# The opening of a decoder trunk kernel: x loaded and normalized ahead of the first modulation weights, those weights in groups of 4, 2 and 2 chunks, weight units split by rows instead of columns, and a shorter chain for the decay rates

## The chip, the cores and the metric

The kernel runs on one core of one Trainium2 chip. The metric is the device time of one execution in microseconds; smaller is better. The time before is the median of three runs, 1262.42 us (1261.84 to 1265.04).

## The reference: what is computed

One inference step of a two-layer decoder trunk on 576 token rows of width 1024: a prompt of 512 rows and 8 samples of 8 rows. All tensors are float32. Around the change, only the beginning matters:

```
def modulate(h, shift, scale):
    return h * (1 + scale[:, None, :]) + shift[:, None, :]

sh1, sc1, g1, sh2, sc2, g2 = split(silu(c) @ ada_w[l] + ada_b[l], 6)    # c: 9 rows (1 prompt, 8 samples)
h = modulate(rms_norm(x, norm_g[l, 0]), sh1, sc1)
xr, yg = split(h @ rnn_w_in, 2)                                          # 1024 x 2048
xr, new_buf = causal_dwconv(xr, conv_buf, conv_w, conv_b)                # width 4
g = einsum('btnc,ncd->btnd', xr blocks, gate_w) + gate_b                 # 8 blocks of 128 x 256
log_a = 8 * sigmoid(g_r) * log_sigmoid(lam)                              # lam: the decay rates, 1024 numbers
...                                                                      # scan, gelu branch, w_out, residual, SwiGLU, attention, SwiGLU
```

So nothing of the first large product, `h @ rnn_w_in`, can be finished before the shift and scale of layer 0 are known for all 1024 features, and these need 2 x 1024 x 1024 numbers of `ada_w` (8.4 MB).

## The kernel before, in words

**Tiling.** Features stand on the 128 partitions, in `KC` = 8 chunks `c` of 128; tokens run along the free dimension in two halves `h` = 0, 1 of 288 columns (256 of the prompt, 32 of the samples). A large product is split into a high and a low part of both operands: per chunk of 128 features three matmuls of 128x128 weights with 128x288 columns (`product`). One output column block of 128 features in one half is 24 such matmuls into one PSUM bank, tile `mm`. There are 6 banks `mm` and 2 banks `ada`. The modulated activations stand in a tile `h` per half, high and low part.

**Weights.** A `Unit` is 512 KB of weights. `load_more` issues its DMA into a `raw` tile (4 of these); `convert` makes the high part on ScalarE (`CAST wh<-raw`) and the low part on VectorE (`TENSOR_TENSOR wh<-raw,wh`) into two `wh` tiles (10 of these). Before, a unit of `rnn_w_in` is one column block with all 8 chunks of rows, in runs of 512 bytes; the two units of the gate weights are each one half of every block's columns.

**The opening.** `x_load` issues the DMAs of the five x tiles (the samples, 4 tiles of 128 prompt rows) into `reg` tiles (5 of these). `x_half(h)` sums the squares, makes the reciprocal root (`acc`, after `spread`), and turns the x tiles with TensorE into `x[h]`. The shift and scale weights of layer 0 come in four groups of two chunks. `ada_first_load(c, ...)` issues 8 DMAs of 256 KB for a group, `ada_first(c)` multiplies them with silu(c) (`cz`, 9 columns padded to 32) in 32 matmuls of 128 columns into a bank `ada`, turns the result with TensorE (`mm<-ident,ta`), and adds the bias into `mods` (`ada_end`). `modulated` then does, chunk by chunk and half by half: normalize (`ta<-x,acc`), scale and shift on ScalarE (`ACTIVATE tb<-ta,mods`), high part on ScalarE (`CAST h<-tb`), low part on VectorE or GpSimd (`h<-tb,h`). The x tiles of half 1 are loaded behind the first group of weights and turned after its modulation. `decay_rates` computes softplus of `lam` with a range reduction, a polynomial and a series: some 90 small VectorE instructions on 128x8 numbers (`sl<-sl`).

**Order.** The program is first recorded as a list of operations. A planner (`Recorder.schedule`) then places them with its own costs and wait times, earliest possible start first, lower program position preferred (`early(n)` moves a piece n positions ahead), and fixes the order of the instructions on each engine: TensorE (PE), VectorE (DVE), ScalarE (ACT), GpSimd (POOL) and the DMA issues on SyncE (SP). On the chip each engine follows that order strictly, so an instruction that waits holds all that stand behind it. Since the planner issues everything, nearly every row of the profile has the one line L447 (L453 in the changed kernel). Rows are told apart by their tiles. The names there: `reg` x tiles or modulation weights, `wh` weight parts or modulation weights, `raw` loaded units, `ada<-wh,cz` and `ada<-reg,cz` modulation products, `mm<-h,wh` the products of h with `rnn_w_in`, `mm<-ident,..` turns.

## Time and profile before

| | |
|---|---|
| median of 3 runs | 1262.42 us |
| the profiled execution's own time | 1263.01 us |
| its span | 1261.2 us, 1.8 us less than its time |
| TensorE busy | 1237.8 us (98%) |
| VectorE, ScalarE, GpSimd busy | 920.3, 663.1, 252.7 us |
| DMA | 165.38 MB, 131 GB/s over the span |
| first product of h, `mm<-h,wh` | begins at 20.71 us |
| first 512-column modulation product, `ada<-reg,cz` | begins at 56.87 us |

Times in the trace count from the start of the span. A row of the timeline gives start, length, engine, operation, tiles, how often it repeats and, in brackets, the engine's idle time before it with what ended it. Lengths of matmuls overlap, since they are pipelined; the distance from start to start is the rate. A float32 matmul (the modulation products) stands in the trace as two records. The windows view gives, for stretches of time, busy us and number of records of each engine, the granted TensorE clock (1.00 is full), the share of the DMA engines and the GB/s moved.

### The profile page before, as it was taken

To read this page: it belongs to the slowest core of one execution; us is meant where nothing else is said; L and a number is where in the kernel's file an instruction comes from. 1 tells how busy PE (TensorE), PEld (TensorE's weight loads), DVE (VectorE), ACT (ScalarE), POOL (GpSimd) and SP (SyncE) were. 2 spreads that over 40 slices of the span, in tenths; PEclk is the share of its full clock that TensorE was granted. 3 is DMA by queue.
4 is the path that set the end of the run, shared out by engine and by line. 5 is a ranking of instruction groups with operands and counts; after the bars stand their busy time and mean duration, and the time that the engine had idled before them with its cause. 6 is when DMAs were issued, how large, how long until landed. Compare 5 with 4: busy or idle time off the path is not lost.

```text
span 1261.2 us, 25276 instructions
## 1 busy us (share of the span) xinstructions
PE 1237.8 (98%) x9532; PEld 1166.9 (93%) x9532; DVE 920.3 (73%) x2283; ACT 663.1 (53%) x1498; POOL 252.7 (20%) x542
## 2 busy tenths in 40 slices
PE   7999999999999999999999999999999999999997
PEld 5798999899899899989998997999999999999997
DVE  6998784795577468656778887558957865875776
ACT  4788973764255335514567678538523542552442
POOL 3456351101100010011024335100011011001011
PEclk8999999999999999999999999999999999999999
DMA  9955554535456655464513220332342232332322
GB/s 306 318 179 188 188 177 151 170 86 171 140 152 191 185 167 184 156 194 137 167 33 75 68 60 27 111 97 97 85 133 68 84 110 76 90 100 80 100 69 76
DMA packets 219755, 165.38 MB, mean 131 GB/s; under 512 B 23629, under 2 KB 204841, under 8 KB 219602
## 3 DMA queue, kind: packets, MB, share of 16 engines
q1 hardware_dynamic: 219186, 163.45, 43.0%
q8 instruction: 75, 1.23, 0.4%
q0 software_dynamic: 448, 0.32, 0.1%
q14 instruction: 46, 0.38, 0.1%
HBM read 160.85 MB, written 4.87 MB: 131 GB/s over the span
## 4 chain that ended last, share of the span: by engine, by line
PE 86%; DVE 6%; ACT 4%; DMA 2%; POOL 1%; issue 1%; SPq 0%; ACTq 0%; DVEq 0%
PE mm L447 82%; PE ada L447 4%; DVE wh L447 1%; DVE ta L447 1%; ACT tb L447 1%; DVE sl L447 1%; ACT ta L447 1%; DVE tb L447 1%; ACT h L447 1%; DMA raw<-in_rnn_w_in_dram 1%; ACT wh L447 1%; POOL h L447 1%; DMA reg<-in_ada_w_dram 1%; ACT sl L447 1%; DMA reg<-in_x_prompt_dram 1%
## 5 line engine op out<-in xcount | busy, mean ns | idle before, releaser
L447 PE MATMUL mm<-h,wh 128*128 128x288 f32 x4128 | 596.2, 298 | 3.8 <-ACT h L447 1.8
L447 PEld LDWEIGHTS mm<-h,wh 128*128 128x128 f32 x4128 | 560.5, 188 | 23.2 <-issue 11.3
L447 PE MATMUL mm<-sl,wh 128*128 128x288 f32 x3218 | 460.6, 296 | 0.4 <-ACT sl L447 0.3
L447 ACT CAST wh<-raw 128x512 fp32r<-128x512 f32 (+2 forms) x380 | 269.1, 721 | 345.7 <-PE mm L447 208.9
L447 PEld LDWEIGHTS mm<-sl,wh 128*128 128x128 f32 x3218 | 436.6, 188 | 9.0 <-issue 5.9
L447 DVE TENSOR_TENSOR wh<-raw,wh 128x512 fp32r<-128x512 f32 (+2 forms) x380 | 310.2, 828 | 59.3 <-ACT wh L447 57.0
L447 DVE SCALAR_TENSOR_TENSOR x<-mm,mods,x 128x256 f32<-128x256 f32 x160 | 77.0, 482 | 136.1 <-PE mm L447 136.0
L447 POOL TENSOR_TENSOR td<-td,td 128x288 f32<-128x288 f32 x38 | 35.5, 934 | 475.8 <-ACT td L447 467.7
L447 POOL TENSOR_TENSOR x<-x,ta 128x32 f32<-128x32 f32 x152 | 55.3, 364 | 331.1 <-DVE ta L447 325.9
L447 PE MATMUL mm<-tb,wh 128*128 128x288 f32 (+1 forms) x488 | 88.5, 296 | 0.4 <-ACT td L447 0.4
L447 PEld LDWEIGHTS mm<-tb,wh 128*128 128x128 f32 x488 | 72.4, 188 | 1.9 <-DVE sl L447 0.8
L447 ACT COPY td<-mm 128x288 f32<-128x288 f32 (+2 forms) x140 | 49.0, 364 | 37.7 <-DVE mm L447 18.0
L447 DVE TENSOR_TENSOR raw<-raw,raw 128x512 f32<-128x512 f32 x76 | 61.4, 808 | 0.9
L447 PE MATMUL mm<-ta,wh 128*128 128x288 f32 (+1 forms) x254 | 56.1, 298 | 0.0
L447 ACT ACTIVATE ta<-x 128x288 f32<-128x288 f32 x56 | 24.8, 444 | 55.6 <-POOL x L447 52.4
L447 DVE TENSOR_TENSOR raw<-raw 128x512 f32<-128x512 f32 x76 | 52.2, 688 | 1.1
L447 DVE TENSOR_TENSOR td<-mm,td 128x288 f32<-128x288 f32 x76 | 34.5, 454 | 23.4 <-PE mm L447 23.3
L447 PE MATMUL ada<-reg,cz 128*32 128x512 f32 (+1 forms) x448 | 49.5, 553 | 0.0
L447 PEld LDWEIGHTS mm<-ta,wh 128*128 128x128 f32 x254 | 41.7, 188 | 1.8 <-ACT wh L447 0.8
L447 ACT ACTIVATE ta<-ta,stat 128x128 f32<-128x128 f32 (+2 forms) x72 | 32.3, 471 | 18.5 <-DVE stat L447 17.7
L447 DVE TENSOR_TENSOR acc<-acc,ta 128x288 f32<-128x288 f32 x54 | 25.1, 464 | 12.4 <-ACT ta L447 12.4
L447 ACT CAST sl<-ta 128x288 fp32r<-128x288 f32 x54 | 23.0, 431 | 18.5 <-DVE ta L447 18.5
(202 smaller groups left out, 1197.9 us busy)
## 6 DMA issues: line engine op xcount, KB each, us to landing
raw<-in_ffn_w_in_dram SPq DMA_DIRECT2D x88, 512.0 KB
reg<-in_ada_w_dram SPq DMA_DIRECT2D x80, 512.0 KB
raw<-in_ffn_w_out_dram SPq DMA_DIRECT2D x48, 384.0 KB
raw<-in_rnn_w_in_dram SPq DMA_DIRECT2D x16, 512.0 KB
reg<-in_kv_ada_w_dram SPq DMA_DIRECT2D x16, 512.0 KB
wh<-in_ada_w_dram SPq DMA_DIRECT2D x24, 256.0 KB
raw<-in_rnn_w_out_dram SPq DMA_DIRECT2D x8, 512.0 KB
raw<-in_ffn_w_out_dram SPq DMA_DIRECT2D x8, 512.0 KB
```

Source lines behind the costliest of these rows:

```text
L447: self.rec.add(eng, lambda: getattr(obj, name)(*map(real, args), **{k: real(v) for k, v in kw.items()}), cost, outs, ins, func, lat, port, ...
```

## The change

- All five x tiles are loaded first; both halves are turned and normalized before any modulation weight is needed. The normalized chunks are kept in 18 `sl` tiles (`X0`), and `modulated` starts from them (`known=True`).
- The first modulation weights come in groups of 4, 2 and 2 chunks (`FIRST`). The group of 4 comes in 8 DMAs of 512 KB with runs of 2 KB, and is multiplied in 32 matmuls of 256 columns; the others as before in 32 matmuls of 128 columns each. A group's matmuls are bound together in three batches (`FQ`: the row quarters 0 and 1, then 2, then 3), so that the planner puts nothing between those of one batch. The result is turned in a bank `ada` (`own`), not `mm`.
- The `rnn_w_in` units of x0 to x3 each hold two column blocks and half the rows (`unit_two`, runs of 1 KB; job `linear_two`). The two gate units each hold both halves of four blocks (1 KB runs), so the first can be dropped earlier.
- `decay_rates` uses ScalarE's Exp and fused operations: 21 or 22 instructions.
- The planner's costs for DMAs now depend on the run length, and one for the modulation matmuls changes.

```diff
-ST = (1, 1, 1)
-EW = EP = EA = EK = E1 = ER = 0
+ST = (2, 1, 2)
+CONV = (1, 1, 1)
+KIND = (0, 1, 0)
+FQ = ((0, 1), (2,), (3,))
+FIRST = ((0, 4), (4, 2), (6, 2))
+EW = EP = EA = EK = ER = 0
+E1 = ((400, 200), (0, 0), (0, 0))
...
-    for t in (4, 0, 1):
+    for t in (4, 0, 1, 2, 3):
         x_load(t)
...
     def decay_rates():
...
-        for kk in (64, 32, 16, 8, 4, 2, 1):
...
-        for n in range(11, 0, -1):
...
+        V.tensor_tensor(p_, lamT, neg, ALU.min)
+        S.activation(p_, p_, AF.Exp)
...
+        for n in range(15, 1, -2):
+            V.scalar_tensor_tensor(s_, s_, 1.0 / n, w2, ALU.add, ALU.mult)
...
-    def ada_first(c):
+    def ada_first(c, n):
         o = ps(pada, "ada")
-        for q, b in enumerate(first_w[c]):
-            for k in range(2):
-                ada_mm(o, 2 * q + k, [b.f[:, n : n + P] for n in (256 * k, 256 * k + P, 512 + 256 * k, 512 + 256 * k + P)], q + k == 0, q + k == 4)
-            b.done()
-        t = ada_turn(o, 1)[:, 0:P].rearrange("p (g c b) -> p g c b", g=2, c=2)
...
+        w = n * P // 2
+        for qs in FQ:
+            with rec.together():
+                for q, k in ((q, k) for q in qs for k in range(2)):
+                    bs = first_w[c][q]
+                    ada_mm(o, 2 * q + k, [bs[g % len(bs)].f[:, (512 * g) % (1024 // len(bs)) + (2 * k + i) * w :][:, 0:w] for g in (SH1, SC1) for i in range(2)], q + k == 0, q + k == 4)
...
+        t = ada_turn(o, n // 2, True)[:, 0 : n * P // 2].rearrange("p (i g f b) -> p g f i b", i=n // 2, g=2, f=2)
...
+    ug = [Unit(KC, [(ALL, slice(0, 4), ALL2, gw[4 * j : 4 * j + 4].rearrange("n p d -> p n d"))]) for j in range(2)]
...
+    def linear_two(us, col, ops, evac):
+        def run(h):
+            o = ps()
+            product(o[:, 0:HC], us[0], ops(h)[0:4], last=False, col=col)
+            product(o[:, 0:HC], us[1], ops(h)[4:8], first=False, col=col)
+            with early(ER):
+                evac(h, o)
+        jobs.append(Job(0.369 * KC, run, us, us))
...
+        if w[0] == "x" and c < 4:
+            if c % 2 == 0:
+                pair[c] = tuple(unit_two(w_in, c * P, k, 4) for k in (0, 4))
+            linear_two(pair[c - c % 2], c % 2 * P, hops, evac_xr(c))
...
+        X0[h] = [sl() for _ in range(KC + 1)]
+        V.tensor_tensor(X0[h][KC].f[:, 0 : 32 * KC].rearrange("p (c n) -> p c n", c=KC), x[h][:, :, HP:HC], rstd[h][:, HP:HC].unsqueeze(1).to_broadcast([P, KC, 32]), ALU.mult)
+        for c in range(KC):
+            (V, V, G)[c % 3].tensor_tensor(X0[h][c].f[:, 0:HP], x[h][:, c, 0:HP], rstd[h][:, 0:HP], ALU.mult)
...
     x_half(0)
-    ada_first_load(0, whs)
+    x_half(1)
+    load_more(1)
+    ada_first_load(*FIRST[0], whs)
     vectors()
-    load_more(1)
-    for t in (2, 3):
-        x_load(t)
     H[0], H[1] = hkind[0](F32R), hkind[1](F32R)
-    for c in range(0, KC, 2):
-        if c < 6:
+    for i, (c, n) in enumerate(FIRST):
+        if CONV[i]:
             convert()
-        ada_first(c)
-        if c < 6:
-            load_more(ST[c // 2])
-            ada_first_load(c + 2, (whs, regs, whs)[c // 2])
+        ada_first(c, n)
+        if i + 1 < len(FIRST):
+            ada_first_load(*FIRST[i + 1], (whs, regs)[KIND[i + 1]])
+            load_more(ST[i])
         for h in range(2):
-            with early(E1):
-                modulated(h, SC1, SH1, M1, slice(c, c + 2))
-            if c == 0 and h == 0:
-                x_half(1)
+            with early(E1[i][h]):
+                modulated(h, SC1, SH1, M1, slice(c, c + n), X0[h], True)
```

How the change moves instructions shows at two places. The first is SP's queue of DMA issues after the first two x tiles. Before (a row `128x2x256 x2` is two DMAs of 256 KB; `x_prompt` rows are 512 KB, `rnn_w_in` rows 512 KB):

```order
L447 DMA reg_111<-in_x_prompt_dram 128x1024
L447 DMA reg_113<-in_x_prompt_dram 128x1024
L447 DMA sl_116<-in_ada_b_dram 96x128
L447 DMA sl_118<-in_norm_g_dram 32x128
L447 DMA wh_121<-in_ada_w_dram 128x2x256 x2
L447 DMA wh_127<-in_ada_w_dram 128x2x256 x2
L447 DMA wh_137<-in_ada_w_dram 128x2x256 x2
L447 DMA wh_147<-in_ada_w_dram 128x2x256 x2
L447 DMA raw_160<-in_rnn_w_in_dram 128x8x128
L447 DMA reg_166<-in_x_prompt_dram 128x1024
L447 DMA reg_173<-in_x_prompt_dram 128x1024
```

Now:

```order
L453 DMA reg_107<-in_x_prompt_dram 128x1024
L453 DMA reg_109<-in_x_prompt_dram 128x1024
L453 DMA reg_112<-in_x_prompt_dram 128x1024
L453 DMA reg_114<-in_x_prompt_dram 128x1024
L453 DMA sl_117<-in_ada_b_dram 96x128
L453 DMA sl_120<-in_norm_g_dram 32x128
L453 DMA raw_124<-in_rnn_w_in_dram 128x4x256
L453 DMA wh_131<-in_ada_w_dram 128x2x512
L453 DMA wh_135<-in_ada_w_dram 128x2x512
L453 DMA wh_140<-in_ada_w_dram 128x2x512
L453 DMA wh_146<-in_ada_w_dram 128x2x512
```

Two more x tiles and a unit now stand ahead of the first modulation weights, and four more rows like the last follow (8 DMAs of 512 KB in place of 8 of 256 KB), then the group of chunks 4 and 5 (2.1 MB), two units, and the group of chunks 6 and 7. Up to and with the last modulation weight of the opening, three units stand in this queue now; before there were three of `rnn_w_in` and one of the gates.

The second place is TensorE's order around the last modulation group of the opening. Before (`ada_661` is that group's bank, `mm_349`, `mm_398` and so on are column blocks of `rnn_w_in`):

```order
L447 MATMUL ada_661<-wh_385,cz 32x128 x6
L447 MATMUL mm_349<-h_323,wh_314 128x288
L447 MATMUL ada_661<-wh_446,cz 32x128 x2
L447 MATMUL mm_398<-h_323,wh_383 128x288
L447 MATMUL mm_349<-h_323,wh_314 128x288
L447 MATMUL mm_349<-h_323,wh_325 128x288
L447 MATMUL ada_661<-wh_446,cz 32x128 x6
L447 MATMUL mm_349<-h_323,wh_314 128x288
L447 MATMUL ada_661<-wh_470,cz 32x128 x2
L447 MATMUL mm_349<-h_323,wh_314 128x288
```

Now:

```order
L453 MATMUL ada_585<-wh_351,cz 32x128 x8
L453 MATMUL ada_585<-wh_361,cz 32x128 x8
L453 MATMUL mm_441<-h_432,wh_523 128x288
L453 MATMUL mm_444<-h_432,wh_523 128x288
L453 MATMUL mm_552<-h_432,wh_539 128x288 x2
L453 MATMUL mm_441<-h_432,wh_523 128x288
L453 MATMUL mm_441<-h_432,wh_537 128x288
L453 MATMUL mm_441<-h_432,wh_523 128x288
L453 MATMUL mm_444<-h_432,wh_523 128x288
```

The modulation matmuls of a group stood in pieces of 2 and 6 between single products of h; now 16 stand together, and the other 16 in a second batch further on. Counted in the order, 122 products of h stand ahead of the first 512-column modulation matmul before, and 135 now. Of the modulation matmuls of 128 columns, 96 of the 128 stood behind the first product of h; now 48 do, in batches of 8, 8, 16 and 16, besides 16 more (and the 32 of 256 columns) ahead of it.

83 lines of the change are left out of this document (44 added, 39 removed).

## The prediction

> **What bounds the kernel now.** First the page: the span, TensorE's share, and the slices.
>
> ```profile
> span 1261.2 us, 25276 instructions
> PE 1237.8 (98%) x9532; PEld 1166.9 (93%) x9532; DVE 920.3 (73%) x2283; ACT 663.1 (53%) x1498; POOL 252.7 (20%) x542
> ...
> PE   7999999999999999999999999999999999999997
> ...
> PEclk8999999999999999999999999999999999999999
> DMA  9955554535456655464513220332342232332322
> ```
>
> TensorE is the bound except in the first slice, where the DMA engines are full, and the last, which the change doesn't touch. The windows view by stage says the same:
>
> ```profile
> 0.00:60.00 60.00, 49.15 (x466) 36.09 (x467) 46.46 (x194) 34.99 (x82) 20.58 (x50) 0.94 1.03 311
> 60.00:200.00 140.00, 139.61 (x1047) 127.53 (x1046) 117.70 (x247) 110.63 (x208) 69.48 (x164) 1.00 0.57 182
> ```
>
> From 60 us on TensorE stands still for 0.4 us in 140, and 1047 records in 140 us are 0.134 us each. What the change can bring is therefore the time at which the opening hands over to this saturated stretch. TensorE's timeline of the opening:
>
> ```profile
> 9.31 1.56 PE L447 MATMUL mm<-ident,reg 128*128 128x128 f32 x8 [0.17 <-DMA reg<-in_x_prompt_dram]
> ...
> 19.56 1.06 PE L447 MATMUL mm<-ident,reg 128*128 128x128 f32 x8 [1.75 <-DMA reg<-in_x_prompt_dram]
> 20.71 0.61 PE L447 MATMUL mm<-h,wh 128*128 128x288 f32 x1
> ...
> 34.81 0.66 PE L447 MATMUL mm<-h,wh 128*128 128x288 f32 x3 [1.57 <-ACT h L447]
> ...
> 44.56 0.40 PE L447 MATMUL mm<-h,wh 128*128 128x288 f32 x1
> 44.88 0.41 PE L447 MATMUL ada<-wh,cz 128*32 128x128 f32 x4
> 45.23 0.66 PE L447 MATMUL mm<-h,wh 128*128 128x288 f32 x3
> 45.82 0.64 PE L447 MATMUL ada<-wh,cz 128*32 128x128 f32 x16
> 46.39 0.66 PE L447 MATMUL mm<-h,wh 128*128 128x288 f32 x3
> 46.98 0.63 PE L447 MATMUL ada<-wh,cz 128*32 128x128 f32 x12
> ...
> 48.07 4.67 PE L447 MATMUL mm<-h,wh 128*128 128x288 f32 x32
> 52.95 3.98 PE L447 MATMUL mm<-h,wh 128*128 128x288 f32 x28 [0.21 <-DVE h L447]
> 56.87 1.93 PE L447 MATMUL ada<-reg,cz 128*32 128x512 f32 x16
> 58.72 0.83 PE L447 MATMUL mm<-ta,wh 128*128 128x300 f32 x4
> ```
>
> My mark is 56.87 us: by then 122 products of h are done (the order's count) and all modulation matmuls of the opening; behind it the work is the same in both kernels and TensorE is saturated. So: when does the changed kernel have 122 products done?
>
> **The change part by part.**
>
> *Landing of the first four chunks' weights.* The second prompt tile of x has landed by 9.3 us, in both kernels. Behind it stand now two x tiles (1.05 MB), two vectors (0.07), one unit (0.52) and 4.19 MB of modulation weights: 5.83 MB. The rates of stretches with 1 KB runs alone and with 4 KB runs alone:
>
> ```profile
> 23.00:32.00 9.00, 8.65 (x104) 5.74 (x103) 7.70 (x38) 4.15 (x9) 2.51 (x6) 0.76 1.11 343
> ...
> 48.00:52.00 4.00, 4.00 (x31) 3.85 (x30) 3.45 (x23) 3.30 (x9) 0.00 (x0) 1.00 1.03 394
> ```
>
> At 343 GB/s it takes 17.0 us (landing at 26.3), with the 2 KB runs at 394 it takes 15.4 (24.7). Runs of 2 KB were not seen; I take 370, in the middle: 4.8 + 11.3 = 16.1, landing at 25.5.
>
> *From there to the first product.* Of the last quarter's eight 256-column matmuls some six remain. Eight instructions of 512 columns are the 16 records at 56.87, with the next row at 58.72: 1.85 us with both switches; at 256 columns six are about 0.9. From the copy of a modulation result to the first product the first group took 20.71 - 17.08 = 3.6 us (ScalarE's timeline):
>
> ```profile
> 17.08 0.27 ACT L447 COPY ta<-ada 128x128 f32<-128x128 f32 x1 [3.19 <-PE ada L447]
> ...
> 35.11 1.09 ACT L447 ACTIVATE tb<-ta,mods 128x256 f32<-128x256 f32 x2
> 36.11 0.70 ACT L447 CAST h<-tb 128x256 fp32r<-128x256 f32 x2
> 36.71 1.05 ACT L447 CAST wh<-raw 128x1024 fp32r<-128x1024 f32 x1
> ```
>
> That held one unit's cast (1.05), which now runs earlier, but four chunks' biases take more on VectorE; I keep 3.6 (bounds 2.6 and 4.2). First product: 25.5 + 0.9 + 0.4 + 3.6 = 30.4 us.
>
> *The products.* 122 at 0.134 are 16.4 us.
>
> *Modulation matmuls among them.* Behind the first product stand 48 in four batches. From 45.23 to 46.39 are three products (0.40) and 16 records, which are 8 instructions: 0.76 with both switches. From 44.56 to 45.23, one product and 2 instructions: 0.54. So a small piece costs nearly as much as a batch, and the binding saves. Two batches of 8 are 1.5 us, two of 16 at 0.76 + 0.44 are 2.4; two turns some 0.2 each: 4.3 in all.
>
> *Stalls.* ScalarE needs 0.9 us for a chunk of one half (1.09 + 0.70 for two); TensorE needs 6 x 0.134 = 0.8 for the two columns at hand. The two run nearly level, and ScalarE must also cast units (1.05 each), and VectorE's low part of the third unit (1.22) stands between the bias and the scale of chunks 4 and 5, so that ScalarE waits for it. Bounds 0 and 2.5; I take 1.0 if TensorE runs at full speed, 0.3 if it is slower.
>
> With a full clock: 30.4 + 16.4 + 4.3 + 1.0 = 52.1, a gain of 4.8 us.
>
> *The clock.* TensorE now has less to do before 30 us. The windows view of the light stretch before:
>
> ```profile
> 13.70:17.10 3.40, 2.86 (x43) 1.00 1.14 339
> 17.10:20.60 3.50, 1.45 (x10) 0.99 1.09 346
> 20.60:24.00 3.40, 3.31 (x14) 0.50 1.11 345
> 24.00:27.40 3.40, 3.40 (x28) 0.50 1.11 350
> 27.40:30.80 3.40, 3.40 (x59) 1.00 1.10 348
> ```
>
> A stretch that was busy 1.45 of 3.5 us was followed by half speed for 6.8 us. In the changed kernel TensorE waits for x, then mostly for weights from about 13 to 30 us, so I expect half speed at the first product. That makes the way to it 0.8 longer (31.2) and each product 0.27, twice 0.134, until the clock is back. Products at 31 are no longer broken by turns, as those at 20.7 to 27.4 were, so I take 3.4 us of half speed, half of what the trace had: of it half is lost, 1.7. Sum: 31.2 + 1.7 + 16.4 + 4.3 + 0.3 = 53.9; against 56.87 a gain of 3.0 us. With 6.8 us of it the loss is 3.4 and the gain 1.3.
>
> The Trainium skill bears on this place (TensorE: Matmul & The Clock Gate, part 1, What's actually happening): half rate comes after an idle window of about 3.4 us and ends after one busy window of the same length. By that rule the sum would be the 53.9 above; the trace, with 6.8 us at half speed under nearly full busy time, agrees with the fall and shows twice the length.
>
> *Decay rates, normalizing, turns.* Groups on VectorE between 14 and 54 us:
>
> ```profile
> L447 DVE TENSOR_TENSOR wh<-raw,wh 128x1024 fp32r<-128x1024 f32 x5 | 6.1, 1221 | 0.4 <-DMA reg<-in_ada_w_dram 0.3
> L447 DVE TENSOR_SCALAR sl<-sl 128x8 f32<-128x8 f32 x35 | 5.8, 166 | 0.3
> ...
> L447 DVE SCALAR_TENSOR_TENSOR sl<-sl 128x8 f32<-128x8 f32 x27 | 4.9, 183 | 0.5
> L447 DVE TENSOR_TENSOR sl<-sl 128x8 f32<-128x8 f32 x18 | 3.0, 164 | 0.4
> ```
>
> and over the whole span on ScalarE:
>
> ```profile
> L447 ACT ACT_TABLE_LOAD x22 | 28.2, 1283 | 3.5 <-DMA raw<-in_c_sample_dram 3.1
> ```
>
> VectorE did 80 small instructions, 13.7 us; some 65 of them go, 11 us, and normalizing (18 instructions) moves ahead of 25 us. Both lie beside the weights' DMAs, so I cost them at nothing of their own: they are why ScalarE's 0.9 per chunk, not VectorE, is level with TensorE. Without that, the small instructions would stand among its low parts and could cost up to 2 us. Exp needs a table load (1.28) near 20 us, where ScalarE waits for weights; over the kernel the order has 19 loads in place of 22, off the path.
>
> **The rivals.**
>
> *A, the clock stays up*: short work at 17 to 27 us (turns, batches as quarters land) keeps it. For it: 13.7 to 17.1, busy 84%, kept full speed. Against it: the turns are over by 13 us. 52.1, gain 4.8: 1257.6.
>
> *B, given back behind the mark.* x0 to x3 now all end with the last chunks, so eight evacuations fall on ScalarE and VectorE at once (each three VectorE passes and three on ScalarE), and the gate matmuls stand behind them in TensorE's order. For it, VectorE is nearly without a gap there already, with three columns' passes in a row (its timeline, then the windows view):
>
> ```profile
> 55.09 4.78 DVE L447 SCALAR_TENSOR_TENSOR sl<-td,vecT,sl 128x300 f32<-128x300 f32 x10
> ```
>
> ```profile
> 55.00:60.00 5.00, 5.00 (x39) 3.32 (x38) 4.93 (x12) 5.00 (x16) 4.49 (x13) 1.00 0.89 227
> ```
>
> Against it: TensorE has rows of x3 and 8 instructions of 512 columns in between (13 products and 1.85 us, 3.6 in all). If the gates wait some 3 us, nothing is left: 1262.4.
>
> *C, slower.* The evacuation chain is the bound from the mark on: the two x3 halves' evacuations, 2 x 1.9 us on VectorE (three passes of 0.48 and a low part), come ahead of the first scans, and each gate matmul waits for them, while half speed lasts 6.8 us. The gain of 1.3, less 3.8, less 2 for the next two units' low parts (1.22 each) among them: 4.5 us slower, 1266.9. It decides if the gates wait more than 5.5 us. Against it: three columns' passes stood so before (the row at 55.09), and the gate matmuls at 58.72 began without idle time.
>
> **How the numbers follow.** The profiled execution took 1263.01 us, 0.6 above the median, and 1.8 above its span; the gain is taken from the median. Forecast (half speed at first, gain 3.0): chance 0.43, own range 1257.5 to 1261.1. A 0.25, B 0.22, C 0.10. Prediction 1262.4 - 3.0 = 1259.4 us. About 0.3% (3.8 us) is what a measurement of this kernel tells from no change, so the boundary is 1258.6. A falls mostly on the faster side (0.22), the forecast's better part too (0.2): 0.42 faster; the rest of the forecast, A's remainder and B 0.49; C 0.09 slower. The range takes in the bounds (landing 24.7 to 26.3, chain 2.6 to 4.2, stalls 0 to 2.5, clock 0 to 3.4) and B and half of C: 1255.5 to 1264.5.
>
> **What would show it.** The last weights of the first four chunks are multiplied near 25.5 us; the first product near 31, at distances of 0.27 us if the clock is down; the last modulation batch and turn near 46, two us ahead of the 48.07 above; the first 512-column matmul, with 13 more products ahead of it, at about 55.5. B shows as idle time of TensorE <-ACT ta or DVE tb at 56 to 70. Wrong would be a landing after 27 or a half clock beyond 38.

## The result

| kernel | median us | runs | ratio to the kernel before, 95% interval |
|---|---|---|---|
| before | 1262.13 | 4 | |
| changed | 1255.96 (1254.43 to 1256.40) | 4 | 0.9944 [0.9927, 0.9961] |
| changed, second comparison (before: 1262.63, 21 runs) | 1254.78 (1254.02 to 1255.32) | 5 | 0.9937 [0.9925, 0.9949] |

The change makes the kernel faster by 6.2 us in the first comparison and 7.9 in the second. The forecast was a gain of 3.0 us, less than half of that. Two executions among all runs, of 5055 and 6789 us, are left out of every ratio. One profiled execution took 1255.87 us with a span of 1254.1, 7.1 us less than that of before. The page of the changed kernel:

```profile
span 1254.1 us, 25044 instructions
PE 1230.8 (98%) x9468; PEld 1164.8 (93%) x9468; DVE 910.4 (73%) x2202; ACT 658.3 (52%) x1493; POOL 256.9 (20%) x542
...
PE   6999999999999999999999999999999999999997
...
PEclk8999999999999999999999999999999999999998
```

and its windows by stage:

```profile
0.00:60.00 60.00, 48.34 (x440) 39.20 (x441) 40.77 (x118) 38.13 (x86) 23.89 (x54) 0.94 0.97 319
60.00:200.00 140.00, 139.95 (x1053) 128.33 (x1052) 117.54 (x249) 105.36 (x202) 69.45 (x162) 1.00 0.62 192
```

TensorE does about the same work after 60 us (139.95 of 140 us busy, 139.61 before), so most of the 7.1 us must have arisen ahead of it. TensorE's timeline of the opening:

```profile
26.48 1.06 PE L453 MATMUL ada<-wh,cz 128*32 128x256 f32 x12 [2.28 <-DMA wh<-in_ada_w_dram]
...
28.38 2.16 PE L453 MATMUL ada<-reg,cz 128*32 128x128 f32 x32
30.67 1.73 PE L453 MATMUL mm<-h,wh 128*128 128x288 f32 x7
...
45.22 8.35 PE L453 MATMUL mm<-h,wh 128*128 128x288 f32 x61
53.50 1.92 PE L453 MATMUL ada<-reg,cz 128*32 128x512 f32 x16
55.35 1.38 PE L453 MATMUL mm<-ta,wh 128*128 128x300 f32 x8
```

The last six modulation matmuls of the first four chunks wait 2.28 us for their weights and start at 26.48, the first product at 30.67. From there the view shows no idle time of TensorE. The rows of products up to 53.50 add up to 135 (7, 10, 19, 20, 14, 4, 61), so the 122nd, the forecast's mark, starts at 51.5 us; in the kernel before it started at 56.6. **At the mark the gain is 5.1 us, not 3.0.** The gate matmuls at 55.35 follow without a wait: rival B (eight evacuations at once) and rival C did not happen.

The rest came later. I followed the starts of the same products in both traces (`mm<-h,wh`, counted in order of time):

| milestone | before us | changed us | lead us |
|---|---|---|---|
| 122nd product of h | 56.6 | 51.5 | 5.1 |
| 1000th product of h | 263.7 | 257.8 | 5.9 |
| 3000th product of h | 862.4 | 856.3 | 6.1 |
| last product of h | 1217.7 | 1210.7 | 7.0 |

(From the 122nd to the 1000th product both kernels run the same 160 records of modulation matmuls, though at other places; all of these are over by 614 us.) A second profile of each kernel gave leads of 5.6, 6.4, 7.1 and 7.8 us: the opening gives 5.1 to 5.6, and 2 us more arise behind it, in both pairs. Two of the places in the kernel before, TensorE's timeline:

```profile
171.38 0.79 PE L447 MATMUL mm<-sl,wh 128*128 128x288 f32 x4 [0.34 <-ACT sl L447]
...
913.75 1.06 PE L447 MATMUL mm<-tb,wh 128*128 128x288 f32 x6 [0.41 <-ACT td L447]
```

In the changed kernel the same six matmuls at the end of a feed-forward column stand as `907.05`, without a wait:

```profile
903.72 3.49 PE L453 MATMUL mm<-h,wh 128*128 128x288 f32 x25
907.05 0.95 PE L453 MATMUL mm<-tb,wh 128*128 128x288 f32 x6
```

25 products from 903.72 take 3.33 us and the next starts at once; before, the row at 913.75 came 0.41 us late by the view, and 0.7 by the distance of starts (24 products from 909.82 to 913.75). The second profiles show the same pair: a wait of 0.43 us at 913.44 before, none at 905.69 in the changed kernel. The program there is the same in both kernels; only the planner's order differs.

**The clock.** TensorE's busy time in stretches of 3.4 us (columns: stretch, length, busy us and records, granted clock, DMA share, GB/s):

```profile
14.82:18.23 3.41, 0.45 (x3) 1.00 1.05 387
18.24:21.64 3.40, 3.40 (x30) 0.50 1.05 386
21.65:25.05 3.40, 2.55 (x30) 1.00 1.06 371
25.06:28.47 3.41, 1.72 (x19) 1.00 1.10 351
28.48:31.88 3.40, 3.27 (x37) 0.50 1.09 347
```

A stretch busy 0.45 of 3.4 us, and one busy 1.72, were each followed by half speed for exactly one such stretch; one busy 2.55 was not. The second half-speed stretch ends at 31.9, so it covers 1.2 us of products and not the forecast's 3.4.

### The profile page after: what moved, and what is told of

It reads as the page before. It is cut to its first block, busy times and chain, and to the rows that moved or that the text cites. A ratio compares the mean times of both kernels' runs of the same rounds, so it can differ in the third digit from the quotient of the medians.

```text
span 1254.1 us, 25044 instructions
## 1 busy us (share of the span) xinstructions
PE 1230.8 (98%) x9468; PEld 1164.8 (93%) x9468; DVE 910.4 (73%) x2202; ACT 658.3 (52%) x1493; POOL 256.9 (20%) x542
## 4 chain that ended last, share of the span: by engine, by line
PE 88%; DVE 4%; ACT 3%; DMA 2%; POOL 1%; issue 1%; SPq 0%; ACTq 0%; DVEq 0%; POOLq 0%
PE mm L453 84%; PE ada L453 5%; DMA wh<-in_ada_w_dram 1%; DVE wh L453 1%; ACT tb L453 1%; ACT ta L453 1%; DVE tb L453 1%; DMA raw<-in_rnn_w_in_dram 1%; DVE sl L453 1%; ACT h L453 1%; DVE ta L453 1%; POOL td L453 1%; DVE stat L453 0%; SPq L453 0%; ACT wh L453 0%
## 5 line engine op out<-in xcount | busy, mean ns | idle before, releaser
L453 POOL TENSOR_TENSOR td<-td,td 128x288 f32<-128x288 f32 x38 | 35.4, 932 | 475.0 <-ACT td L453 468.9
L453 POOL TENSOR_TENSOR x<-x,ta 128x32 f32<-128x32 f32 x152 | 58.2, 383 | 325.0 <-DVE ta L453 320.1
L453 ACT ACTIVATE ta<-x 128x288 f32<-128x288 f32 x56 | 24.8, 444 | 54.9 <-POOL x L453 51.7
L453 DVE TENSOR_TENSOR raw<-raw 128x512 f32<-128x512 f32 x76 | 52.3, 689 | 1.1
```

The costliest lines, as they stand in the source:

```text
L453: self.rec.add(eng, lambda: getattr(obj, name)(*map(real, args), **{k: real(v) for k, v in kw.items()}), cost, outs, ins, func, lat, port, ...
```

## Experiments

Each run was compared with the kernel before on the same chip. "Loss" is the ratio less 0.9940 (the mean of the changed kernel's two), times 1262.4 us; its uncertainty is about 1.5 us.

| kernel | median us | ratio, 95% interval | loss us |
|---|---|---|---|
| changed, x2, x3 and the first unit behind the first group | 1260.98 | 0.9988 [0.9979, 0.9997] | 6.1 |
| changed, that and groups of two | 1259.70 | 0.9982 [0.9973, 0.9991] | 5.3 |
| changed, long decay chain | 1260.01 | 0.9978 [0.9967, 0.9990] | 4.8 |
| changed, long decay chain placed late | 1263.96 | 1.0005 [0.9997, 1.0014] | 8.2 |
| changed, groups of two | 1260.04 | 0.9975 [0.9965, 0.9984] | 4.4 |
| changed, x0 to x3 by columns | 1258.56 | 0.9967 [0.9954, 0.9980] | 3.4 |
| changed, batches not bound | 1258.35 | 0.9964 [0.9951, 0.9976] | 3.0 |
| changed, old gate units | 1258.50 | 0.9963 [0.9949, 0.9977] | 2.9 |
| changed, first unit behind the first group | 1256.57 | 0.9950 [0.9938, 0.9962] | 1.3 |
| changed, TensorE kept busy | 1256.01 | 0.9941 [0.9930, 0.9953] | 0.1 |
| changed, another DMA price for the planner | 1255.55 | 0.9942 [0.9930, 0.9954] | 0.3 |
| before, short decay chain alone | 1264.71 | 1.0012 [1.0003, 1.0020] | |
| before, again | 1262.50 | 1.0001 [0.9992, 1.0010] | |

### Is it the clock? TensorE kept busy

```diff
+                for _ in range(4 if 0 in qs else 7):
+                    T.matmul(d[:, 0:256], ident[:], first_w[c][qs[-1]][0].f[:, 0:256], start=True, stop=True)
```

(and eight more behind the turns of the last x tile)

> 19 matmuls of 256 columns with the identity (about 0.43 us each at full speed), whose results nobody reads, fill TensorE's idle time at 14 to 18 and 20 to 26 us; all else is as in the changed kernel, and the outputs are the same. Theory 'clock' (the half speed of 28.5 to 31.9 us comes from the idle time before it and costs 0.6 us in the products and 0.3 ahead of them): the granted clock stays at 1.0 from 11 to 35 us, the first product begins near 30.3 us, products are 0.134 us apart from the first on, and the time is 1255.1, 0.9 less than 1256.0. Rival (clock without worth, since the weights' landing and ScalarE's chain set the opening): the clock stays up and the time is 1255.7 to 1256.5. If the half speed comes whatever TensorE does, the clock row still shows 0.5 near 28 us.

Measured 1256.01 us, ratio 0.9941: no gain, though the time alone, good to 1.5 us, could not tell the 0.9 us of the first theory from none. The clock did stay up (1.00 from 11 to 1250 us):

```profile
25.06:28.47 3.41, 3.12 (x55) 1.79 (x52) 2.23 (x16) 0.45 (x2) 0.34 (x2) 1.00 1.10 348
28.48:31.88 3.40, 2.59 (x37) 1.74 (x35) 2.13 (x7) 3.40 (x10) 0.23 (x1) 1.00 1.10 349
```

and yet the start barely moved:

```profile
24.94 1.93 PE L453 MATMUL ada<-wh,cz 128*32 128x256 f32 x32
...
30.03 1.39 PE L453 MATMUL mm<-h,wh 128*128 128x288 f32 x7 [0.73 <-ACT h L453]
```

The last of the weights landed at 25.6 in this run by the DMA records; the first product starts 4.4 us behind that, with a wait for ScalarE's first chunk. Three profiles give the same: from the start of the last six modulation matmuls to the first product it is 4.19 us in the changed kernel with half speed (26.48 to 30.67), 4.19 in the run with another DMA price (25.23 to 29.42), and 4.19 in its own second profile, which had no half speed there:

```profile
24.97 1.06 PE L453 MATMUL ada<-wh,cz 128*32 128x256 f32 x12 [0.39 <-DMA wh<-in_ada_w_dram]
...
29.16 1.39 PE L453 MATMUL mm<-h,wh 128*128 128x288 f32 x7 [0.63 <-ACT h L453]
```

So what lies between is the chain over ScalarE and VectorE, and TensorE's half speed runs beside it. From the first product to the 122nd it took 20.9 us with half speed and 20.6 without (second profile, and this run). **The clock cost the changed kernel 0.3 us, where the forecast had put 2.5** (1.7 in the products and 0.8 ahead of them; with 0.7 less for stalls, 1.8 more than in rival A). The rival expected here, "clock without worth", holds. As to the length of half speed, the first profile agrees with the rule the prediction weighed, one busy window (the Trainium skill, TensorE: Matmul & The Clock Gate, part 1, What's actually happening): 3.4 us each time. The second profile does not: there it lasted 6.8 us, from 16.9 to 23.8. As to the cause the rows are milder than an idle window, since 1.72 busy of 3.4 us were enough to fall.

### Is it the landing? The first unit behind the first group

```diff
-    load_more(1)
     ada_first_load(*FIRST[0], whs)
+    load_more(1)
```

> The first weight unit (512 KB) is loaded behind the eight DMAs of the first modulation group and not ahead of them; all else is as in the changed kernel. Theory 'landing' (the opening is set by the landing of the first group's last weights): the last of them lands about 1.35 us earlier (25.1 in place of 26.4 us), the first product begins near 29.5 in place of 30.67 us, and the time falls by about 1.2 us, from 1256.0 to 1254.8. Rival 'chain' (the opening is set by ScalarE, which has to convert the unit behind its landing, among the first h chunks): the weights land earlier, the first product doesn't begin earlier than 30.3, and the time is 1256 to 1257.

Measured 1256.57 us: no gain, though the first product began at 27.79, 2.9 us earlier than in the first profile of the changed kernel and 1.4 earlier than in its second. Neither theory had that pair. The windows view and TensorE's timeline:

```profile
29.40:32.70 3.30, 3.30 (x23) 2.99 (x27) 1.87 (x6) 3.30 (x10) 1.61 (x6) 0.50 1.09 348
```

```profile
27.79 0.54 PE L453 MATMUL mm<-h,wh 128*128 128x288 f32 x2 [2.16 <-ACT h L453]
...
29.26 2.90 PE L453 MATMUL mm<-h,wh 128*128 128x288 f32 x11
```

Here TensorE idles 2.16 us ahead of its first product and does little before, and half speed falls on 11 products in a row (2.9 us in place of 1.5) and on the batch between. By the 122nd product the lead over the first profile is 0.25 us, and the second is 1.5 us ahead. So half speed costs some 1.7 us where it falls on products and batches (1.4 on these products, 0.3 on the batch at 32.09); in the changed kernel most of it does not fall there. The rest of what was lost up to the 122nd product I have not traced. Three tries to have both, the early unit and fillers, gave nothing: the fillers held up the last batch or the first product, or the chain did.

The two edits together:

> Both edits of the two earlier runs on the changed kernel: the first weight unit behind the first modulation group, and filler matmuls that keep TensorE busy from 14 to 26 us. Theory (the earlier start of 2.9 us that the unit's place gave was eaten by half speed at 29 to 33 us, so that with a full clock it comes through): the first product near 27.6 us, granted clock 1.0 throughout the opening, the first 512-column modulation matmul at 50.5 to 51.5 in place of 53.5 us, and a time of 1253.3 to 1254.5. Rival (the third group's landing near 41 us holds the opening whatever comes before): TensorE idle near 38 to 44 us, 52.5 us for that matmul, and 1255 to 1256.

Measured 1259.04, slower than either theory had it, first product at 31.43: the fillers behind the third quarter ended at 25.0, 1.4 us after the last weights had landed (23.6 by the DMA records). VectorE then made a unit's low part (1.23 us from 28.87) between two steps of the modulation, and half speed came at 32.4 to 35.8 after all.

With fillers at other places (the unit moved as before):

```diff
+                    for _ in range(8):
+                        T.matmul(d[:, 0:256], ident[:], src[:, 0:256], start=True, stop=True)
...
+                for _ in range(5):
+                    T.matmul(d[:, 0:256], tt_s[0].f[:, 0:P], x[0][:, 0, 0:256], start=True, stop=True)
```

> The changed kernel with the first unit behind the first modulation group, and fillers at two places only: 8 matmuls of 256 columns behind the turns of the last x tile, 5 behind the turn of the first group's result. In the earlier try the fillers in the middle ended at 25.0 us and so held up the last batch, whose weights had landed at 22.9 in the run without fillers. Theory (the gain of 2.9 us at the first product was eaten by half speed): first product near 27.7 us, no half speed between 28 and 40 us, the 122nd product at 49 to 50 in place of 51.5 us, and a time of 1254 to 1255. Rival (half speed comes anyway, or the third group holds the opening): the 122nd at 51 or later, 1255.5 to 1257.

Measured 1255.54, first product 30.04, 122nd at 52.1: no difference to the changed kernel (0.9940). The five fillers behind the turn ran from 26.25 to 29.8, mostly at half speed (25.5 to 28.9), and TensorE could not begin the products before:

```profile
26.25 3.66 PE L453 MATMUL mm<-x,ta 128*128 128x256 f32 x10
```

And with shorter ones at all places (8, 4, 2 and 4):

> The changed kernel with the first unit behind the first modulation group, and shorter fillers that keep TensorE busy from 14 us to the first product: 8, 4 and 2 matmuls of 256 columns behind the last x turns, the first two quarters and the third, and 4 behind the turn. Theory (half speed eats the 2.9 us of an earlier start): granted clock 1.0 from 11 us on, first product at 27.8 to 28.6, 122nd product at 48.8 to 50, time 1253.5 to 1254.8 (0.9920 to 0.9935 of before). Rival (the start is not what holds the opening): full clock, first product early, the 122nd still at 51 or later, time 1255.5 to 1256.5.

Measured 1257.62, above both theories. The clock stayed up from 13 to 780 us, the weights were multiplied by 25.9, and the first product still started at 30.26. VectorE shows why, and ScalarE waits for it:

```profile
28.01 0.16 DVE L453 TENSOR_SCALAR nsp<-sl 128x8 f32<-128x8 f32 x1
28.08 0.42 DVE L453 TENSOR_TENSOR mods<-ada,abT 128x18 f32<-128x18 f32 x4
```

```profile
28.62 1.09 ACT L453 ACTIVATE tb<-sl,mods 128x256 f32<-128x256 f32 x2 [1.32 <-DVE mods L453]
```

The bias addition (`mods<-ada,abT`) could have run behind the turn at 26.8; it stands behind the decay chain, short as it is. In the changed kernel the chain ends at 27.0 and the turn at 28.4, so it is covered, with little to spare. An earlier landing meets this limit next.

### Is it the decay chain?

```diff
     def decay_rates():
...
-        S.activation(p_, p_, AF.Exp)
+        for kk in (64, 32, 16, 8, 4, 2, 1):
...
```

> The decay rates are computed by the long chain of the kernel before (some 90 small VectorE instructions); all else is as in the changed kernel. Forecast's theory (covered by the weights' DMAs, or up to 2 us where they stand among the low parts): 1256.0 to 1258.0, with the 65 further small instructions (11 us) partly between 26 and 50 us, and stalls of TensorE <-DVE h there. Rival (VectorE has room enough): 1255.7 to 1256.4.

Measured 1260.01 us, 4.8 lost. The forecast costed the short chain at nothing and its absence at up to 2 us; **that step fell here.** The profiled execution is a long one (1263.99 us, 4.0 above the median; 2.4 of it is half speed at 786 us, as in the last section), so I read only its opening. ScalarE's timeline with the long chain, and VectorE's:

```profile
30.57 1.09 ACT L453 ACTIVATE tb<-sl,mods 128x256 f32<-128x256 f32 x2 [3.48 <-DVE mods L453]
```

```profile
29.96 0.16 DVE L453 TENSOR_SCALAR sl<-sl 128x8 f32<-128x8 f32 x1
30.03 0.42 DVE L453 TENSOR_TENSOR mods<-ada,abT 128x18 f32<-128x18 f32 x4
```

The modulation result was copied at 26.7, but its bias is added at 30.03, behind small instructions; ScalarE waits 3.48 us (1.07 in the changed kernel, row at 29.03 further below), and the first product starts at 32.21. The remaining small instructions stand among the low parts up to 51.7 us, and a half-speed stretch of 6.8 us falls on the first products. At the mark 4.4 us are lost against the first profile of the changed kernel, 6.1 against the second.

```profile
27.58 0.37 ACT L453 COPY ta<-ada 128x256 f32<-128x256 f32 x1 [3.71 <-PE ada L453]
29.03 1.09 ACT L453 ACTIVATE tb<-sl,mods 128x256 f32<-128x256 f32 x2 [1.07 <-DVE mods L453]
```

Is it the place or the amount? The same long chain, placed later:

```diff
-    with early(100):
+    with early(-300):
```

> The changed kernel with the long decay chain of before, placed 400 positions later in the planner's order, so that it comes behind the additions of the first group's biases on VectorE and not ahead of them. Theory 'place': the bias is added right behind the turn (28.5 us, not 30.0), ScalarE's wait <-DVE mods falls from 3.5 to about 1.1 us, the first product begins near 30.7 and the time is 1256 to 1257.5. Rival 'amount': the small instructions now stand among the low parts, and the time stays at 1259 to 1261.

Measured 1263.96 us, 8.2 lost: "place" fell as I had put it, and "amount" had put 1259 to 1261. The opening is indeed repaired (first product 29.23, the 122nd at 50.5), but the last of the chain's some 85 dependent steps (`nsp<-sl`) runs at 75.1 us, where it ran at 50.9 in the kernel before, and the gate evacuations (`sl<-ta,nsp`) need its result. The first of these starts at 83.5 us, against 70.4 in the kernel before and 60.3 in the changed one. TensorE's timeline:

```profile
105.46 0.54 PE L453 MATMUL mm<-ta,wh 128*128 128x300 f32 x2 [0.76 <-ACT tb L453]
...
107.54 0.60 PE L453 MATMUL mm<-ident,ta 128*128 128x128 f32 x2 [1.40 <-ACT tb L453]
```

followed by a half-speed stretch at 107.7. The long chain thus costs 4 us or more at both places tried in the changed opening. And in the kernel before?

```diff
     def decay_rates():
...
-        for kk in (64, 32, 16, 8, 4, 2, 1):
...
+        S.activation(p_, p_, AF.Exp)
```

> The kernel before with the short decay chain alone (22 instructions in place of some 90). Theory 'place' (the long chain costs where it stands right ahead of a modulation result in VectorE's queue, as in the run of the changed kernel with the long chain; in the kernel before the first result is due at 17 us and the later ones find it in pieces): 1261.4 to 1262.8, no more than 1 us of gain. Rival 'amount' (11 us of VectorE work between 14 and 54 us slow every step of the opening): 1258 to 1259.5, the first 512-column modulation matmul some 3 to 4 us ahead of 56.87 us.

Measured 1264.71 us, slower by 0.12%. At the 122nd product (54.8 us) it led the kernel before's first profile by 1.9 us and its second by 0.7. Up to the 1000th it lost 3.5, most of it at one place:

```profile
148.99 1.15 PE L447 MATMUL mm<-ta,wh 128*128 128x300 f32 x4 [1.92 <-ACT ta L447]
```

```profile
149.30:152.70 3.40, 3.40 (x20) 1.06 (x18) 3.40 (x6) 2.22 (x4) 0.02 (x1) 0.50 0.05 15
```

An idle time of 1.92 us by the view (2.2 by the starts) and, right behind it, half speed for 3.4 us. That is rival B in another kernel: a lead in the opening given back in the gate stage, which is only nearly saturated. "No more than 1 us of gain" was right, though the time lies above the range given, and its reason (results that find the chain in pieces) was not: the opening did gain.

### The other parts, undone one by one

x2 and x3 behind the first group:

```diff
-    for t in (4, 0, 1, 2, 3):
+    for t in (4, 0, 1):
...
     x_half(0)
+    ada_first_load(*FIRST[0], whs)
+    load_more(1)
+    for t in (2, 3):
+        x_load(t)
     x_half(1)
-    load_more(1)
-    ada_first_load(*FIRST[0], whs)
```

> The changed kernel, groups of 4, 2, 2 kept, with x2, x3 and the first unit behind the first modulation group. Theory 'no limit may be left' (the first group's weights land some 4 us earlier, near 20.9 us, but the turns, squares and normalizing of half 1 then stand among the first products on TensorE, VectorE and ScalarE): first product of half 0 at 25 to 26.5 us, TensorE waiting for x or for h of half 1, 122nd product 1 to 4 us later than in the changed kernel (49.8 and 51.5 in its two traces), time 1257 to 1259.5 (0.9955 to 0.9975 of before). Rival (x first brings nothing): 1254.5 to 1256.

Measured 1260.98 us, the largest loss of any part and above the theory's range. The unit that moves with x cost 1.3 us by itself (uncertain by 1.5). The first product starts at 25.6, 3.5 us ahead of the changed kernel's second profile; then TensorE waits for the last x tiles, for chunks and for low parts, partly at half speed, and the 122nd starts at 56.5:

```profile
24.02 1.97 PE L453 MATMUL mm<-ident,reg 128*128 128x128 f32 x8 [2.14 <-DMA reg<-in_x_prompt_dram]
...
36.52 4.98 PE L453 MATMUL mm<-h,wh 128*128 128x288 f32 x26 [2.12 <-ACT h L453]
...
43.72 0.54 PE L453 MATMUL mm<-h,wh 128*128 128x288 f32 x2 [1.64 <-DVE wh L453]
```

Groups of two chunks:

```diff
-FIRST = ((0, 4), (4, 2), (6, 2))
-E1 = ((400, 200), (0, 0), (0, 0))
+FIRST = ((0, 2), (2, 2), (4, 2), (6, 2))
+E1 = ((0, 0), (0, 0), (0, 0), (0, 0))
...
```

> The changed kernel with the first modulation weights in four groups of two chunks (as before the change: 256 KB DMAs, runs of 1 KB, 32 matmuls of 128 columns each) in place of 4, 2, 2. Theory (groups of 4 save two batches' switches and turns and 32 matmuls, and the DMAs with 2 KB runs take 1.35 us per 512 KB against 1.5): the last modulation weights land 0.6 to 1.2 us later, the first product begins earlier (near 23 us, at half clock), TensorE waits for later groups, and the time is 1257.5 to 1259. Rival (the start is what counts, and two chunks land 7 us earlier than four): 1254 to 1256.

Measured 1260.04 us, 1 us above the theory's range. The profiled execution (1257.61) is the fastest of ten and shows less than that loss: first product at 24.58, the 122nd at 52.3. In between, the same:

```profile
31.50 0.53 PE L453 MATMUL mm<-h,wh 128*128 128x288 f32 x2 [1.46 <-ACT h L453]
...
40.02 2.79 PE L453 MATMUL mm<-h,wh 128*128 128x288 f32 x19 [1.64 <-DVE wh L453]
```

An early start is worth little where TensorE runs out of columns behind it. Both edits together:

> The changed kernel with x2 and x3 behind the first modulation group, as before the change, and groups of two chunks: what stays of the change are the bound batches, the half units, the gate units by blocks, the own bank for turns, normalizing ahead and the short decay chain. Theory 'no single part' (each part undone cost 2.4 to 4 us because the opening then meets another limit; what counts is that none is left): 1258.5 to 1261. Rival (the order of x and the groups bring nothing, the other parts all): 1255.5 to 1257. Rival (they bring most): 1261 to 1263.

Measured 1259.70 us, within the first theory's range: 5.3 us lost, which the uncertainty does not tell from the 6.1 of x alone.

x0 to x3 by columns:

```diff
-        if w[0] == "x" and c < 4:
+        if w[0] == "x" and c < 0:
```

> The changed kernel with x0 to x3 loaded by columns as before the change (one column block with all rows, 512 byte runs) and computed one column at a time. Theory 'halves' (units of two columns and half the rows let two columns of two halves start on the first four chunks with only one unit converted, so TensorE has work for all four banks): products run out while the later chunks are missing, the 122nd product is done 1 to 3 us later than at 51.5 us, and the time is 1257 to 1259. Rival (the columns end one after the other, so evacuations and gates spread better): 1255 to 1256.

Measured 1258.56 us; 122nd product at 52.4, and a wait of 0.41 us for GpSimd's low part at 35.4.

Batches not bound:

```diff
-FQ = ((0, 1), (2,), (3,))
+FQ = ((0,), (1,), (2,), (3,))
...
-            with rec.together():
+            if True:
```

> The changed kernel without the binding of a group's modulation matmuls into batches: the planner may again put products between them. Forecast's theory (a small piece costs nearly as much as a batch: 0.54 against 0.76 us): some 6 to 10 pieces in place of 4 behind the first product, 1.5 to 2.5 us more at the mark, and 1257.5 to 1258.5. Rival (the planner's new price keeps them together anyway): 1255.5 to 1256.5.

Measured 1258.35 us, as the forecast's own reasoning had it: ten pieces of 2 to 14 instructions (4 to 28 records) behind the first product in place of four batches. TensorE's timeline shows the first of them, part of it at half speed:

```profile
30.12 0.64 PE L453 MATMUL ada<-reg,cz 128*32 128x128 f32 x4
30.70 1.33 PE L453 MATMUL mm<-h,wh 128*128 128x288 f32 x4
31.96 1.06 PE L453 MATMUL ada<-reg,cz 128*32 128x128 f32 x12
```

The gate units of the kernel before:

```diff
-    ug = [Unit(KC, [(ALL, slice(0, 4), ALL2, gw[4 * j : 4 * j + 4].rearrange("n p d -> p n d"))]) for j in range(2)]
+    ug = [Unit(KC, [(ALL, slice(0, KC), ALL, gw[:, :, t * P : (t + 1) * P].rearrange("n p d -> p n d"))]) for t in range(2)]
...
```

> The changed kernel with the two gate units as before the change (each one half of every block's columns, 512 byte runs, both kept until the last gate). Theory 'gates' (the two units by blocks let the first be dropped early and need only one of them converted ahead of the first gates, which is why the changed kernel, unlike the kernel before with the short chain, keeps its gain of the first 55 us through the gate stage): the first 512-column modulation matmul stays at 52.5 to 54 us, but TensorE waits <-ACT ta or tb between 60 and 165 us for 1 to 3 us, and the time is 1257.5 to 1260. Rival (the units' shape is worth nothing): 1255.5 to 1256.7.

Measured 1258.50 us. Its opening is as good as any (122nd product at 49.9), and 2.6 us go in the gate stage. The waits view of the page shows no idle TensorE there, though; the windows of 120 to 180 us do, first for the changed kernel's second profile, then for this one:

```profile
120.00:180.00 60.00, 60.00 (x455) 54.90 (x457) 52.41 (x110) 45.70 (x84) 30.89 (x72) 1.00 0.57 172
```

```profile
120.00:180.00 60.00, 59.86 (x439) 53.50 (x438) 51.14 (x104) 45.29 (x83) 28.70 (x70) 1.00 0.57 178
```

Both are "busy" for 60 us, but 455 records against 439: at 0.134 us each, 16 records are 2.1 us. The weight loads show part of what the matmul rows hide (engine PEld, waits of this run):

```profile
PEld mm L453 <- ACT ta L453: 1.4, 3, 0.8
PEld mm L453 <- DVE ta L453: 0.8, 1, 0.8
```

All waits of `mm` weight loads there are 3.7 us, and 2.4 in the changed kernel's second profile. The starts of the products give the whole: from the 122nd to the 1000th it is 208.8 us here and 206.2 there.

### Scatter and the planner's order

One number of the planner, its DMA price for long runs:

```diff
-... else 345.0) + 5
+... else 340.0) + 5
```

> Only a number of the planner is changed: its price of a DMA with long runs (340 in place of 345 bytes per ns), which moves some 370 rows of the order and no work. Theory 'order' (the 2 us that the changed kernel gained behind the first 60 us come from the order that the planner happened to find): the time differs from 1256.0 by 0.5 to 1.5 us in either direction, and the difference arises behind 60 us. Rival (that gain comes from the change itself): 1255.8 to 1256.3.

Measured 1255.55 us (0.9942): no difference that can be told. At the mark this run leads the first profile by 1.5 us, 1.25 of it from the landing (its last six matmuls start at 25.23, not 26.48) and 0.26 from the products, which had no half speed here. It is one other order; others may differ by more.

The two kernels again, unchanged, for a second profile each:

> The changed kernel as it is, on this chip, with a second profile. If the first trace was typical: time 1255.5 to 1256.5 (0.9930 to 0.9955 of the kernel before on the same chip), first product near 30.7, 122nd product at 51 to 52 us, and the lead over the kernel before 5 us at 60 us, 6 at 300 us and 7 at the end. If one DMA engine's late packet (the last quarter of the first group at 26.4 us, 2.4 us behind most engines) was chance: landing near 25.0, first product at 29.3, 122nd at 50.2, and the difference does not reach the end in full.

Measured 1254.78; first product 29.16, 122nd at 49.8. So the 26.4 us of the first profile was a late one.

> The kernel before as it is, with a second profile. If its first trace was typical: 122nd product at 56 to 57.5 us, 500th product at 126 to 127 us, and no half speed between 60 and 1250 us. If the 2 us behind the mark are scatter, the distance from the 122nd product to the end (1204.6 us in the first trace, 1202.6 in that of the changed kernel) comes out 1 us or more shorter.

Measured 1262.50; 122nd product at 55.4, 500th at 125.2. From the 122nd to the 500th product it is 69.7 us in both profiles of before and 67.8 in both of the changed kernel, but there the kernel before runs 16 more records of modulation matmuls (80 against 64), which are 1.85 us. Up to the 1000th the work is equal: 207.0 us in both of before, 206.2 and 206.3 in the changed kernel. From the 122nd to the last it is 1161.0 and 1161.7 us against 1159.2 and 1159.5, and 0.7 of the 1161.7 is half speed at 785 us. So 0.8 us up to the 1000th product repeat exactly, and the other 1.1 to 1.3 come near the scatter.

## Why the prediction was right or wrong

- **What bounds the kernel, and the mark**: right. The time went down because TensorE reaches the 122nd product earlier; the mark gave 5.1 of 7.1 us (5.6 of 8.0 in the second pair).
- **Landing of the weights**: forecast 25.5 (24.7 to 26.3). The last matmuls started at 26.48 and 24.97; the mean is right, the first profile just outside.
- **Landing to first product**: forecast 4.9 us at full clock and 5.7 with half speed; measured 4.2 with either, so this term was 0.7 too long even without the clock.
- **The clock**: this step failed in its size. In the first profile half speed did fall on the time around 30 us; it cost 0.3 us, not 2.5, because most of it lay beside the chain on ScalarE and on modulation matmuls. In the second profile, and in the run with another DMA price, it was over by 23.8, so that it came as forecast was in part chance. Rival A's sum, 52.1 us, is what came: 51.5 and 49.8. I had argued half speed from TensorE's busy share and then charged it as if TensorE were the bound ahead of its first product. In the first profile the way from 53.9 to 51.5 is: landing 1.0 later, landing to first product 1.5 shorter (4.2 for 5.7), first product to the 122nd 1.8 shorter (20.9 for 22.7). That the sum of A came out so near is in part luck: in that profile its landing was 1.0 too early and its chain 0.7 too long.
- **Modulation matmuls and stalls**: from the first product to the 122nd 20.6 us at full clock, of which 121 distances of 0.134 are 16.2: 4.4 for batches, turns and stalls, against 4.3 and up to 1.0. The view shows no idle time, so the stalls were small.
- **"Behind it the work is the same in both kernels and TensorE is saturated"**: this step failed. The work is the same, its order is not, and 2 us more came from there. The runs show the stretch up to some 260 us to be saturated only if its gates are fed in time: from the 122nd to the 1000th product it gave 0.8 us in the changed kernel, took 3.5 in the kernel before with the short chain, and against the changed kernel it took 2.6 with the old gate units and 7.3 with the late long chain. Some 0.7 to 0.9 us more came behind the 3000th product, the wait near 910 us among them; which detail of the new order saved them was not tested.
- **Decay rates and normalizing at nothing, "without it up to 2 us"**: failed. With the long chain the changed kernel loses 4.8 us, without x ahead 6.1. This did not make the forecast miss, since the change has the short chain; it priced wrongly what the change is worth. (Normalizing ahead and the turn in a bank of its own were not undone by themselves.) The cover named (the weights' DMAs) covers VectorE's time, not its order: a dependent chain ahead of the bias addition delays every later step, and one behind it delays the gates.
- **B and C**: did not happen here. B's mechanism is real and appeared in two of the experiments.

What the parts are worth cannot be added up. The six losses of single parts sum to 24.6 us, while the whole change gains 6.2 to 7.9; one part alone, the short chain, gains nothing. Each part takes away a limit that would otherwise hold the opening or the gate stage, so undoing any one brings that limit back. No tried version is measurably faster than the changed kernel.

## What to carry to other kernels

Before charging a slower TensorE to a stretch, find what its first dependent instruction waits for: here half speed beside a chain on ScalarE and VectorE cost nothing, and on a run of products half of its time. A long chain of tiny dependent instructions has two deadlines, the first important instruction queued behind it and the first reader of its result, so its busy time is not its price. And where several limits stand level, test a part by undoing it in the changed kernel, not by adding it to the old one; the two gave opposite answers here.

## What was not expected of the hardware

**One late DMA engine.** In the first profile half of the 16 landing signals of the first group's last DMA had come by 24.0 us and 15 of them by 24.8. The last one came at 26.4, and one signal then stayed some 2.4 us behind the median for every DMA up to 45 us. Between 23 and 24 us the DMA view has a packet of another queue:

```profile
q1 hardware_dynamic: 276, 0.36, 101.2%
q8 instruction: 1, 0.02, 6.8%
```

One packet of 16 KB of instructions, 6.8% of 16 engine-microseconds, held one engine for 1.1 us. It accounts for most of the step from 0.9 to 2.4 us of lag; that the two belong to the same engine I infer from the times. The next such packet, of 1.12 us at 38.29, fits: from the DMA that ended at 41.3 on a second signal is 2.1 us late, 0.9 before. The Trainium skill (Runtime: NRT & Kernel Launch, Instruction fetch mechanics) says that such 16 KB refills are mostly hidden; for the engine that issues, they may be, but here, by these times, the landing of a weight batch waited for it.

**Half speed in the middle of the program.** In 9 of the 19 profiles, of the kernel before and of variants of both, one stretch of 3.4 or 6.8 us at half speed begins at 780 to 788 us, in the attention stage. The windows view of the second profile of before:

```profile
785.60:788.90 3.30, 3.30 (x15) 2.04 (x16) 2.67 (x13) 2.90 (x12) 1.15 (x2) 0.50 0.57 169
```

It comes or not with the same program, costs 0.7 us (the lead of this profile over the first falls from 1.0 to 0.3 us across it) and 1.6 and 2.4 in two profiles where it is twice as long, and may make up part of the scatter of 1 to 3 us between runs of one kernel. Busy share does not explain it: the stretch of 3.4 us ahead of it was busy for 2.9 to 3.0 us in all nine, while stretches busy for 2.4 us near 685 us kept full speed in many profiles. What decides stays open.
